# Projections beside an attention stage, in steps of three matmuls behind each of 64 blocks

## Chip, cores and metric

The kernel runs on one core of a Trainium2 chip. The metric is the device time of one execution in microseconds (us), lower is better. The kernel before takes 1805.41 us (median of 3 runs, 1805.12 to 1806.67).

## What is computed

Two layers on 512 tokens of width 1024, everything in float32. Each layer normalizes, projects, and adds three branches: an attention of eight heads in two groups (compressed keys, selected keys, a window), a retention and a causal convolution of 31 taps with a norm of its own. Each branch is projected and multiplied by a gate:

```python
h = _rmsnorm(x, norm_mix[l])
z = h @ w_in[l]
o_nsa = _nsa(q_n, kc, vc, ks, vs, kw, vw, g_n, ...)
o_ret = _retention(q_r, k_r, v_r, g_r, ret_gn[l])
o_conv = _conv_module(c_a, c_b, conv_w[l], ...)
proj = jnp.einsum('bsnc,ncd->bsnd', br, w_branch[l])
gate = jax.nn.sigmoid(m_g).reshape(B, S, N_BRANCH, D_MODEL)
x = x + jnp.sum(gate * proj, axis=2) @ w_out[l]
x = x + jnp.square(jax.nn.relu(_rmsnorm(x, norm_mlp[l]) @ w_ff1[l])) @ w_ff2[l]
```

## The kernel before

Every float32 operand is split into a high and a low part, and each step of 128 rows in a projection is three matmuls (high by high, high by low, low by high) of 128x512. A projection from width 1024 (`proj`) has 8 steps, 24 matmuls; one from width 512 has 4 steps, 12 matmuls. SP loads a block of weights (`wr`), ACT rounds its high part (`wh`, L145), POOL takes the difference (`wl`, L148). PSUM's eight banks are pools by name: three `mm`, two `sc`, two `tp`, one `av`. The program is written for a scheduler that fixes the order of each engine ahead of time; `tc.issue_after(x)` says that what is written under it is to be issued no sooner than instruction x.

In a layer the order is: convolution input and retention, compressed keys and values, keys, values V (four accumulators of 128x280, `proj_tok`), `query(0)`, then the attention. The attention has four head pairs (`attention_pair`, j = 0 to 3), each with four passes (two groups g, two branches br), 16 passes in all. A pass has four blocks (i = 0 to 3), 64 blocks in a layer. For each block PE makes two score matmuls into an `sc` bank (128 to 512 columns), DVE adds the bias and takes the minimum (L712), ACT the exponential (L714). After the fourth block's sum DVE works out the scale (`gate_over`, L627 to L629), ACT applies it to each block (L719), PE transposes the block into a `tp` bank (L722), and ACT and DVE copy it out as high and low part (L727, L728). Eight `av` matmuls end the pass. Each pair also has a small softmax over compressed keys (`pc`, L673 to L690) at its head. `query(j + 1)` is projected during pair j.

DVE also makes the convolution's taps (L338, 0.7 to 0.9 us each), dealt behind the blocks by `conv_taps_behind`; the generator `conv_norm` (L590 to L612) follows from pass 12 on, a piece per pass. What fills PE beside the attention is the list `pending`: eight `mix` items (gate of 24 matmuls, projection of 12) and sixteen `gate_ahead` items (24). One is done before the keys, four (`HELD`) are kept for the end; the other 19 are dealt whole over the passes:

```python
u = 4 * j + k
with tc.issue_after(marks[u].ins):       # the pass's first score matmul
    fill(paced * (u + 1) // 16 - paced * u // 16)
```

Each item ends with a DVE multiply out of its `mm` bank (L448, and L464 for the second half of a `mix`). After the last pass the `os` projections begin, which need all of the attention.

Of the kernel before, what the change touches and what calls it, by code (L numbers as in the profile page):

```python
# [2 lines left out]

# [14 lines left out]
P = 128  # L18
# [3 lines left out]
KC = D // P  # L22
# [11 lines left out]
FB_CA, FB_CB, FB_GR, FB_KC, FB_VC, FB_KS, FB_KW, FB_MG, FB_Q = 0, 4, 8, 12, 13, 14, 15, 16, 40  # L34
# [32 lines left out]
def block_kernel(ctx: ExitStack, tc: tile.TileContext, a, out):  # L67
    nc = tc.nc
# [12 lines left out]
    AHEAD, F_KEYS, HELD = 16, 1, 4  # L81
# [18 lines left out]
    def ps(tag, shape=(P, T)):  # L100
        return tl(psum, tag, PS_BUFS[tag], shape)
# [6 lines left out]
    def mm(o, l, r, start, stop):  # L108
        return nc.tensor.matmul(o, l, r, start=start, stop=stop)  # L109
# [43 lines left out]
    def wblock(src, nk=KC, n=P):  # L153

        return wsplit(raw(lambda t: [(t, src)], nk, n), nk, n)

    def proj(o, w, x, nk=KC):

        h, l = w
        for k in range(nk):  # L160
            xh, xl = x[k]
            mm(o, h[:, k, :], xh, k == 0, False)
            mm(o, h[:, k, :], xl, False, False)
            last = mm(o, l[:, k, :], xh, False, k == nk - 1)
        return last

    def proj_tok(outs, srcs, n, x, shared=1):

# [101 lines left out]
    for l in range(DEPTH):  # L270
# [49 lines left out]
        def conv_taps_behind(ins, n):  # L320
            with tc.issue_after(ins.ins):
                conv_taps(n)
# [118 lines left out]
        merged = [None] * KC  # L441
        gated = set()

        def gate(n, m):
            pg = ps("mm")
            proj(pg, wblock(w_f[FB_MG + n * KC + m]), X)
            t = tl(base, "g", 3)
            nc.vector.tensor_mul(t, pg, rs)  # L448
            nc.scalar.activation(t, t, AF.Tanh, scale=0.5)
            return t  # L450

        def gate_ahead(n, m):
            dma(gdram[n * KC + m], gate(n, m))
            gated.add((n, m))

        def mix(n, o, m):
            if (n, m) in gated:
                t = tl(base, "g", 3)
                dma(t, gdram[n * KC + m])
            else:  # L460
                t = gate(n, m)
            po = ps("mm")
            proj(po, wblock(a["w_b"][l, n, m], 4), o, 4)
            nc.vector.scalar_tensor_tensor(t, t, 1.0, po, op0=OP.add, op1=OP.mult)  # L464
            if n == 1:
                dma(mdram[m], t)
            else:
                nc.vector.tensor_add(merged[m], merged[m], t)

        pending = [lambda m=m: mix(1, RO, m) for m in range(KC)]  # L470
        pending += [lambda k=k: gate_ahead(2 * (k // KC), k % KC) for k in range(AHEAD)]
        paced = len(pending) - F_KEYS - HELD

        def fill(n):
            for _ in range(min(n, len(pending))):
                pending.pop(0)()


        phase.close()
# [84 lines left out]
            conv_taps_behind(low, T_KEYS)  # L564
        G = tl(mix_pool, "G", 1, (P, NB, 24))
        V = []
        pz = [ps(tag) for tag in ("mm", "mm", "mm", "av")]
        proj_tok([p[:, :280] for p in pz], [(a["w_v"][l][:, k0:k0 + nk], nk) for k0, nk in ((0, 3), (3, 3), (6, 2))], 280, X)
        for i in range(NB):
            v = kv((P, 4, P))  # L570
# [80 lines left out]
        def attention_pair(j, tq, more):  # L651
# [43 lines left out]
            for g in range(2):  # L695
                h = g * HPG + j
                nat, oth = halves(g)
                av = ps("av")
                mm(av, vcb[:, g, :], pct, True, False)
                for br in range(2):  # L700
                    den, mx = small((P, NB)), small((P, NB))
                    S = tl(ap, "s", 3, (P, 1280))
                    cols = []
                    for i in range(NB):
                        n = P * (i + 1)
                        sc = ps("sc")
                        m0 = mm(sc[:, :n], QS[g][:, i * P:(i + 1) * P], KHH[br, g][:, :n], True, False)
                        if i == 0:
                            marks.append(m0)
                        mm(sc[:, :n], QS[g][:, i * P:(i + 1) * P], KLL[br, g][:, :n], False, True)  # L710
                        s = S[:, 64 * i * (i + 1):64 * i * (i + 1) + n]
                        nc.vector.tensor_tensor_reduce(s, sc[:, :n], bias[g][:, 384 - 128 * i:512], scale=1.0,  # L712
                                                       scalar=3e38, op0=OP.add, op1=OP.min, accum_out=mx[:, i:i + 1])
                        nc.scalar.activation(s, s, AF.Exp, scale=-1.0, bias=mx[:, i:i + 1], accum_out=den[:, i:i + 1])  # L714
                        cols.append(s)
                    c = gate_over(den, h, 1 + br)
                    ph, pl = tl(ap, "pt", 4, (P, 1280), FR), tl(ap, "pt", 4, (P, 1280), FR)
                    for i in range(NB):
                        nc.scalar.activation(cols[i], cols[i], AF.Copy, scale=c[:, i:i + 1])  # L719
                        pt = ps("tp")  # L720
                        for k in range(i + 1):
                            nc.tensor.transpose(pt[:, k * P:(k + 1) * P], cols[i][:, k * P:(k + 1) * P], ident)  # L722
                        for (vh, ks), (vl, _) in zip(pt_views(ph, i), pt_views(pl, i)):
                            src = pt[:, ks.start * P:ks.stop * P]
                            if len(vh.shape) == 3:
                                src = src.rearrange("p (k q) -> p k q", q=P)
                            nc.scalar.activation(vh, src, AF.Copy)  # L727
                            low = nc.vector.tensor_sub(vl, src, f(vh))  # L728
                        slot = 4 * (4 * j + 2 * g + br) + i
                        conv_taps_behind(low, late_taps * (slot + 1) // T_SLOTS - late_taps * slot // T_SLOTS)  # L730
                    for k, c0 in enumerate((0, 512, 896, 1152)):
                        n = T - k * P
                        lhs = V[k][:, 2 * br + g, :]
                        mm(av[:, k * P:], lhs, ph[:, c0:c0 + n], False, False)
                        mm(av[:, k * P:], lhs, pl[:, c0:c0 + n], False, br == 1 and k == NB - 1)
                    more(j, 2 * g + br)
                t = tmp()
                nc.scalar.activation(t[nat], av[oth], AF.Copy)
                nc.vector.tensor_add(oj[nat], t[nat], av[nat])
            return oj  # L740

        ON, marks, tqs = [], [], [query(0)]
        late_taps = len(todo)

        def more(j, k):

            if k == 0 and j + 1 < HPG:
                tqs.append(query(j + 1))
            if not todo:
                next(normed, None)  # L750
            u = 4 * j + k
            with tc.issue_after(marks[u].ins):
                fill(paced * (u + 1) // 16 - paced * u // 16)

        for j in range(HPG):
            ON.append(attention_pair(j, tqs[j], more))
        conv_taps(len(todo))
        for _ in normed:
            pass
        with tc.issue_after(marks[-1].ins):  # L760
            fill(len(pending))

        phase.close()
        phase = ExitStack()
# [123 lines left out]
```

## Time and profile before

| | |
|---|---|
| median of 3 runs | 1805.41 us |
| the profiled execution, its own time | 1804.74 us |
| its span (first to last instruction) | 1803.0 us |
| mean granted TensorE clock | 0.984 of full |
| PE (matmul) busy | 1757.3 us, 97% |
| DVE busy | 1104.4 us, 61% |
| ACT busy | 774.9 us, 43% |
| POOL busy | 500.6 us, 28% |

Ends of matmuls are modelled, and a matmul that waits in the pipeline counts as busy, so PE's busy time is more than the time it needs; the spacing of starts is a better measure. In layer 0 `query(0)` begins at 205.10 us, the first block is transposed at 241.60, the first `os` projection starts at 465.09; in layer 1 these are 1094.81, 1125.04 and 1348.92.

### The profile page before, as it was taken

What the parts mean: (1) busy time and instruction counts of PE and PEld (TensorE: products, weight loads), DVE (VectorE), ACT (ScalarE), POOL (GpSimd) and SP (SyncE); (2) the same over time, 40 slices, a digit from 0 to 9 for tenths busy, and PEclk for the clock granted to TensorE, in tenths of its full rate; (3) what the DMA queues carried; (4) which work ended last, traced back from release to release, by engine and by line L of the source; (5) the groups of instructions that cost most, each with busy time, mean ns of one, the idle gap of its engine ahead of it and who ended that gap; (6) DMA issues with size and microseconds to landing.
All of it is one profiled execution on the core that took longest, in us unless ns stands there. A gap on an engine that the chain in (4) does not pass through costs nothing.

```text
span 1803.0 us, 23260 instructions
## 1 busy us (share of the span) xinstructions
PE 1757.3 (97%) x8592; PEld 1473.8 (82%) x8592; DVE 1104.4 (61%) x1979; ACT 774.9 (43%) x1421; POOL 500.6 (28%) x420
## 2 busy tenths in 40 slices
PE   8899899989999999999999999999899999999997
PEld 7788788868888888888898888888688888888886
DVE  6976978887554344434459778878857443434344
ACT  4433466766343232323434344667553341323241
POOL 4454444323471000000255543343137500000000
PEclk9999999989999999999999999999899999999998
DMA  4222623221753323333422232332147323332321
GB/s 167 87 88 61 203 94 122 96 71 65 233 169 96 101 96 93 95 96 102 135 94 89 87 127 83 98 131 90 41 161 227 119 94 94 93 94 94 105 85 68
DMA packets 70802, 195.82 MB, mean 109 GB/s; under 512 B 8945, under 2 KB 9329, under 8 KB 70689
## 3 DMA queue, kind: packets, MB, share of 16 engines
q1 hardware_dynamic: 70688, 194.34, 33.6%
q8 instruction: 68, 1.11, 0.3%
q14 instruction: 46, 0.37, 0.1%
HBM read 177.51 MB, written 19.42 MB: 109 GB/s over the span
## 4 chain that ended last, share of the span: by engine, by line
PE 67%; issue 20%; DVE 10%; ACT 2%; DMA 1%; SPq 0%; POOLq 0%; POOL 0%; DVEq 0%; ACTq 0%
PE mm L109 58%; PE sc L109 3%; DVE yc L338 3%; PE av L109 3%; PE tp L722 2%; PE tp L109 1%; DVE XP L500 1%; DVE kv L563 1%; DVE qk L386 1%; ACT s L719 0%; DVE pt L728 0%; ACT wh L145 0%; DVE rr L364 0%; PE tp L190 0%; DVE s L712 0%
## 5 line engine op out<-in xcount | busy, mean ns | idle before, releaser
L109 PE MATMUL mm<-X,wh 128*128 128x512 f32 x2432 | 777.4, 396 | 12.2 <-ACT X L214 6.1
L148 POOL TENSOR_TENSOR wl<-wr,wh 128x512 fp32r<-128x512 f32 (+2 forms) x344 | 436.2, 1290 | 563.2 <-ACT wh L145 540.6
L145 ACT ACTIVATE wh<-wr 128x1024 fp32r<-128x1024 f32 (+2 forms) x301 | 296.9, 987 | 681.9 <-PE mm L109 554.5
L109 PEld LDWEIGHTS mm<-X,wh 128*128 128x128 f32 x2432 | 455.3, 189 | 103.1 <-ACT X L214 6.3
L109 PE MATMUL mm<-X,wl 128*128 128x512 f32 x1216 | 479.5, 394 | 0.4 <-DVE wl L150 0.4
L109 PEld LDWEIGHTS mm<-X,wl 128*128 128x128 f32 x1216 | 230.2, 189 | 46.5 <-DVE wl L150 0.9
L338 DVE SCALAR_TENSOR_TENSOR yc<-u,ccol,yc 128x512 f32<-128x512 f32 x240 | 214.2, 894 | 1.7
L150 DVE TENSOR_TENSOR wl<-wr,wh 128x1024 fp32r<-128x1024 f32 x129 | 158.1, 1225 | 38.4 <-ACT wh L145 38.4
L109 PE MATMUL mm<-fa,wh 128*128 128x512 f32 x512 | 160.2, 395 | 0.0
L109 PE MATMUL mm<-bo,wh 128*128 128x512 f32 x512 | 160.0, 391 | 0.0
L805 DVE SCALAR_TENSOR_TENSOR t<-mm,rs 128x512 f32<-128x512 f32 x64 | 43.9, 691 | 161.5 <-PE mm L109 155.9
L227 POOL TENSOR_TENSOR t<-t,t 128x512 f32<-128x512 f32 x18 | 27.4, 1523 | 333.7 <-DVE wl L150 310.7
L206 POOL TENSOR_TENSOR n<-n,mhalf 128x4 f32<-128x4 f32 x15 | 16.5, 1101 | 372.3 <-DVE n L204 372.3
L109 PE MATMUL mm<-kv,wh 128*128 128x512 f32 x384 | 119.5, 389 | 0.0
L109 PEld LDWEIGHTS mm<-fa,wh 128*128 128x128 f32 x512 | 96.1, 188 | 23.2
L109 PEld LDWEIGHTS mm<-bo,wh 128*128 128x128 f32 x512 | 96.0, 188 | 19.7
L109 PE MATMUL mm<-fa,wl 128*128 128x512 f32 x256 | 100.5, 395 | 0.0
L109 PE MATMUL mm<-bo,wl 128*128 128x512 f32 x256 | 100.2, 392 | 0.0
L714 ACT ACTIVATE s<-s,n 128x128 f32<-128x128 f32 (+3 forms) x128 | 71.4, 559 | 46.9 <-DVE n L712 46.3
L109 PE MATMUL mm<-wh,X 128*128 128x256 f32 (+1 forms) x480 | 90.1, 286 | 0.0
L728 DVE TENSOR_TENSOR pt<-tp,pt 128x128 fp32r<-128x128 f32 (+1 forms) x192 | 70.0, 372 | 32.7 <-ACT pt L727 32.4
L816 DVE TENSOR_TENSOR yc<-yc,mm 128x512 f32<-128x512 f32 x32 | 22.0, 687 | 105.6 <-PE mm L109 105.6
(219 smaller groups left out, 2463.9 us busy)
## 6 DMA issues: line engine op xcount, KB each, us to landing
wr<-in_w_dram SPq DMA_DIRECT2D x128, 512.0 KB, 3.5
wr<-in_w_f_dram SPq DMA_DIRECT2D x87, 512.0 KB, 3.3
wr<-in_w_b_dram SPq DMA_DIRECT2D x48, 256.0 KB, 2.7
wr<-in_w_t_dram SPq DMA_DIRECT2D x16, 512.0 KB, 3.4
gd<-g SPq DMA_DIRECT2D x32, 256.0 KB, 2.0
g<-gd SPq DMA_DIRECT2D x32, 256.0 KB, 2.8
wr<-in_w_o_dram SPq DMA_DIRECT2D x16, 512.0 KB, 3.6
md<-g SPq DMA_DIRECT2D x16, 256.0 KB, 2.9
```

The lines of the kernel that those rows point to most:

```text
L109: return nc.tensor.matmul(o, l, r, start=start, stop=stop)
L145: nc.scalar.activation(h, t, AF.Copy)
L148: nc.gpsimd.tensor_sub(l[:, k], t[:, k], f(h[:, k]))
L150: nc.vector.tensor_sub(l, t, f(h))
L227: (nc.vector if c == KC - 1 or first_time else nc.gpsimd).tensor_add(s, s, acc)
L338: nc.vector.scalar_tensor_tensor(yc[c], x, w, yc[c], op0=OP.mult, op1=OP.add)
L386: nc.vector.tensor_sub(QLr[h][half], pt[nat], f(QHr[h][nat]))
L714: nc.scalar.activation(s, s, AF.Exp, scale=-1.0, bias=mx[:, i:i + 1], accum_out=den[:, i:i + 1])
L722: nc.tensor.transpose(pt[:, k * P:(k + 1) * P], cols[i][:, k * P:(k + 1) * P], ident)
L728: low = nc.vector.tensor_sub(vl, src, f(vh))
L805: nc.vector.scalar_tensor_tensor(t, pf, 0.0, rs, op0=OP.max, op1=OP.mult)
L816: nc.vector.tensor_add(xT[m], xT[m], pf)
```

## The change

`proj` becomes a loop over a generator, `proj_steps`, which yields after each three matmuls. `gate`, `mix` and `gate_ahead` become generators as well. The 19 items (7 `mix` of 12 steps, 12 `gate_ahead` of 8, 180 steps, 540 matmuls) are chained into one generator, `beside`, and 2 or 3 steps are drawn after each of the 64 blocks, to be issued behind that block's last transpose. The four held items follow after the last pass, no longer behind the last pass's first score. V's second and third accumulators take the two `sc` banks in place of two `mm` banks. Line numbers after L160 shift by 5 to 17.

```diff
     def proj(o, w, x, nk=KC):
 
+        for _ in proj_steps(o, w, x, nk):
+            pass
+
+    def proj_steps(o, w, x, nk=KC):
+
         h, l = w
         for k in range(nk):
             xh, xl = x[k]
             mm(o, h[:, k, :], xh, k == 0, False)
             mm(o, h[:, k, :], xl, False, False)
-            last = mm(o, l[:, k, :], xh, False, k == nk - 1)
-        return last
+            mm(o, l[:, k, :], xh, False, k == nk - 1)
+            yield
...
         def gate(n, m):
+            w = wblock(w_f[FB_MG + n * KC + m])
             pg = ps("mm")
-            proj(pg, wblock(w_f[FB_MG + n * KC + m]), X)
+            yield from proj_steps(pg, w, X)
...
-        pending = [lambda m=m: mix(1, RO, m) for m in range(KC)]
-        pending += [lambda k=k: gate_ahead(2 * (k // KC), k % KC) for k in range(AHEAD)]
-        paced = len(pending) - F_KEYS - HELD
+        pending = [(12, mix_steps(1, RO, m)) for m in range(KC)]
+        pending += [(8, gate_ahead(2 * (k // KC), k % KC)) for k in range(AHEAD)]
...
-        pz = [ps(tag) for tag in ("mm", "mm", "mm", "av")]
+        pz = [ps(tag) for tag in ("mm", "sc", "sc", "av")]
...
-                        m0 = mm(sc[:, :n], QS[g][:, i * P:(i + 1) * P], KHH[br, g][:, :n], True, False)
-                        if i == 0:
-                            marks.append(m0)
+                        mm(sc[:, :n], QS[g][:, i * P:(i + 1) * P], KHH[br, g][:, :n], True, False)
...
-                            nc.tensor.transpose(pt[:, k * P:(k + 1) * P], cols[i][:, k * P:(k + 1) * P], ident)
+                            turned = nc.tensor.transpose(pt[:, k * P:(k + 1) * P], cols[i][:, k * P:(k + 1) * P], ident)
...
+                        with tc.issue_after(turned.ins):
+                            for _ in range(paced * (slot + 1) // 64 - paced * slot // 64):
+                                next(beside)
...
+        paced = sum(n for n, _ in pending[:-HELD])
+        beside = itertools.chain(*(steps for _, steps in pending[:-HELD]))
...
-            u = 4 * j + k
-            with tc.issue_after(marks[u].ins):
-                fill(paced * (u + 1) // 16 - paced * u // 16)
...
-        with tc.issue_after(marks[-1].ins):
-            fill(len(pending))
+        for _ in beside:
+            pass
+        del pending[:-HELD]
+        fill(HELD)
```

The first place is PE's order at the head of the attention in layer 0, between the score matmuls of the first two passes (`sc`) and the first block's transpose (`tp<-ident,s`). `mm<-X` and `mm<-bo` are matmuls of the list. Before:

```order
L109 MATMUL sc_393_2200<-kv_337_1882,QS_373_2131 128x384
L109 MATMUL sc_393_2200<-kv_338_1883,QS_373_2131 128x384
L109 MATMUL sc_394_2205<-kv_337_1882,QS_373_2131 128x512
L109 MATMUL sc_394_2205<-kv_338_1883,QS_373_2131 128x512
L690 MATMUL tp_384_2177<-ident_66,pch_383_2174 128x128 x4
L109 MATMUL sc_419_2352<-kv_346_1931,QS_373_2131 128x128
L109 MATMUL sc_419_2352<-kv_347_1932,QS_373_2131 128x128
L109 MATMUL mm_430_2421<-X_12_115,wh_432_2424 128x512
L109 MATMUL mm_430_2421<-X_13_116,wh_432_2424 128x512
L109 MATMUL mm_430_2421<-X_12_115,wl_433_2425 128x512
```

After, up to the first block's transpose and the first matmuls of the list behind it:

```order
L705 MATMUL tp_384_2177<-ident_66,pch_383_2174 128x128 x4
L110 MATMUL sc_421_2357<-kv_346_1931,QS_373_2131 128x384
L110 MATMUL sc_421_2357<-kv_347_1932,QS_373_2131 128x384
L110 MATMUL sc_422_2362<-kv_346_1931,QS_373_2131 128x512
L110 MATMUL sc_422_2362<-kv_347_1932,QS_373_2131 128x512
L110 MATMUL av_387_2185<-pct_385_2182,vc_322_1785 128x512
L110 MATMUL sc_444_2478<-kv_339_1888,QS_375_2136 128x128
L110 MATMUL sc_444_2478<-kv_340_1889,QS_375_2136 128x128
L735 MATMUL tp_398_2217<-ident_66,s_390_2189 128x128
L110 MATMUL mm_402_2229<-X_12_115,wh_400_2224 128x512
L110 MATMUL mm_402_2229<-X_13_116,wh_400_2224 128x512
L110 MATMUL mm_402_2229<-X_12_115,wl_401_2225 128x512
```

Before, 87 matmuls of the list and of the second query stand between `query(0)` and the first block's transpose; now none does, and the first six stand behind that transpose.

The second place is PE's order in pass 10 of layer 0. Before, the list has run out by here, and no matmul of it stands in the 73 rows from the end of pass 9 to that of pass 13:

```order
L722 MATMUL tp_676_3724<-ident_66,s_666_3683 128x128 x3
L109 MATMUL sc_747_4107<-kv_346_1931,QS_708_3935 128x128
L109 MATMUL sc_747_4107<-kv_347_1932,QS_708_3935 128x128
L109 MATMUL sc_748_4112<-kv_346_1931,QS_708_3935 128x256
L109 MATMUL sc_748_4112<-kv_347_1932,QS_708_3935 128x256
L109 MATMUL av_663_3679<-pct_616_3421,vc_322_1785 128x512
L722 MATMUL tp_677_3734<-ident_66,s_666_3683 128x128 x4
L109 MATMUL av_663_3679<-pt_672_3708,kv_364_2068 128x512
L109 MATMUL sc_749_4117<-kv_346_1931,QS_708_3935 128x384
L109 MATMUL sc_749_4117<-kv_347_1932,QS_708_3935 128x384
L109 MATMUL sc_750_4122<-kv_346_1931,QS_708_3935 128x512
L109 MATMUL sc_750_4122<-kv_347_1932,QS_708_3935 128x512
```

After, the same pass, with the list's steps behind each block:

```order
L735 MATMUL tp_680_3738<-ident_66,s_665_3667 128x128 x3
L110 MATMUL mm_679_3730<-X_16_123,wh_677_3725 128x512
L110 MATMUL mm_679_3730<-X_17_124,wh_677_3725 128x512
L110 MATMUL mm_679_3730<-X_16_123,wl_678_3726 128x512
L110 MATMUL mm_679_3730<-X_18_127,wh_677_3725 128x512
L110 MATMUL mm_679_3730<-X_19_128,wh_677_3725 128x512
L110 MATMUL mm_679_3730<-X_18_127,wl_678_3726 128x512
L110 MATMUL sc_711_3926<-kc_307_1699,tq_641_3541 128x64 x4
L110 MATMUL sc_725_3975<-kv_337_1882,QS_707_3916 128x128
L110 MATMUL sc_725_3975<-kv_338_1883,QS_707_3916 128x128
L110 MATMUL av_662_3663<-pct_610_3375,vc_322_1785 128x512
L735 MATMUL tp_681_3754<-ident_66,s_665_3667 128x128 x4
```

Six or nine matmuls of the list now stand behind each block's transposes, in all 64 blocks.

The third place is PE's order where the convolution's norm begins (`mm<-ones` sums columns, `mm<-ident,n` spreads the mean over rows), at the end of pass 13. Before:

```order
L109 MATMUL mm_759_4172<-ones_71,u_737_4063 128x1 x4
L109 MATMUL av_722_3989<-pt_752_4131,kv_364_2068 128x512
L109 MATMUL av_722_3989<-pt_753_4132,kv_364_2068 128x512
L109 MATMUL av_722_3989<-pt_752_4131,kv_365_2072 128x384
L109 MATMUL av_722_3989<-pt_753_4132,kv_365_2072 128x384
L190 MATMUL mm_760_4178<-ident_66,n_758_4171 128x128 x4
L109 MATMUL mm_765_4198<-X_12_115,wh_767_4201 128x512
L109 MATMUL mm_765_4198<-X_13_116,wh_767_4201 128x512
L109 MATMUL mm_765_4198<-X_12_115,wl_768_4202 128x512
L109 MATMUL mm_765_4198<-X_14_119,wh_767_4201 128x512
```

After, from the mean's spreading to the first transpose of pass 14:

```order
L196 MATMUL mm_769_4225<-ident_66,n_767_4218 128x128 x4
L110 MATMUL sc_781_4263<-kv_339_1888,QS_709_3921 128x384
L110 MATMUL sc_781_4263<-kv_340_1889,QS_709_3921 128x384
L110 MATMUL sc_782_4268<-kv_339_1888,QS_709_3921 128x512
L110 MATMUL sc_782_4268<-kv_340_1889,QS_709_3921 128x512
L110 MATMUL av_775_4248<-pct_719_3967,vc_322_1785 128x512
L110 MATMUL sc_801_4374<-kv_348_1937,QS_709_3921 128x128
L110 MATMUL sc_801_4374<-kv_349_1938,QS_709_3921 128x128
L110 MATMUL sc_802_4379<-kv_348_1937,QS_709_3921 128x256
L110 MATMUL sc_802_4379<-kv_349_1938,QS_709_3921 128x256
L735 MATMUL tp_786_4280<-ident_66,s_778_4252 128x128
L110 MATMUL mm_766_4206<-X_14_119,wh_764_4201 128x512
```

Before, a whole gate stands behind the mean's spreading; now the last scores of pass 14 and its first transpose stand there, with no matmul of the list in between.

## Rows read from the trace of the kernel before

**Rows 1.** The page's first lines: span, then busy time by engine
```profile
span 1803.0 us, 23260 instructions
PE 1757.3 (97%) x8592; PEld 1473.8 (82%) x8592; DVE 1104.4 (61%) x1979; ACT 774.9 (43%) x1421; POOL 500.6 (28%) x420
```

**Rows 2.** Busy time by stretch: start and end, length, engines, clock, DMA, GB/s
```profile
205.10:241.60 36.50, 36.09 (x173) 30.38 (x174) 29.92 (x76) 15.40 (x37) 12.29 (x12) 0.91 0.37 117
...
241.60:381.06 139.46, 139.46 (x725) 118.11 (x724) 115.79 (x315) 96.34 (x240) 54.73 (x44) 1.00 0.33 108
...
381.06:412.31 31.25, 24.23 (x112) 18.07 (x110) 27.15 (x77) 19.41 (x55) 2.64 (x2) 0.78 0.08 27
...
1094.81:1125.04 30.23, 29.83 (x142) 24.66 (x141) 24.59 (x66) 15.34 (x36) 12.09 (x12) 0.99 0.27 83
...
1264.30:1296.12 31.82, 25.07 (x112) 18.93 (x110) 27.43 (x77) 19.30 (x55) 2.63 (x2) 0.73 0.08 26
```

**Rows 3.** The chain that ended last: start, length, engine, line, instructions
```profile
455.66 105.57 PE mm L109 x461
```

**Rows 4.** Busy time by stretch of five microseconds, columns as before
```profile
205.00:210.00 5.00, 4.90 (x12) 3.85 (x13) 5.00 (x9) 1.98 (x6) 2.97 (x2) 0.50 0.81 272
210.00:215.00 5.00, 5.00 (x21) 4.06 (x20) 4.82 (x7) 0.64 (x1) 0.59 (x1) 0.87 0.19 54
...
400.00:405.00 5.00, 4.17 (x16) 2.75 (x14) 3.67 (x7) 2.26 (x6) 0.00 (x0) 0.50 0.00 0
...
1090.00:1095.00 5.00, 5.00 (x24) 5.00 (x24) 4.88 (x9) 1.16 (x5) 0.72 (x2) 0.50 0.62 205
```

**Rows 5.** PE's timeline: start, length, operation, idle time before it and releaser
```profile
205.10 1.22 PE L109 MATMUL mm<-X,wh 128*128 128x512 f32 x2 [4.69 <-ACT G L575]
...
395.38 0.66 PE L722 MATMUL tp<-ident,s 128*128 128x128 f32 x4 [1.54 <-DVE pt L728]
...
442.70 0.51 PE L722 MATMUL tp<-ident,s 128*128 128x128 f32 x3
442.97 0.48 PE L109 MATMUL mm<-X,wl 128*128 128x512 f32 x1
```

**Rows 6.** DVE's timeline in layer 0, from the first query to the first gate
```profile
209.24 7.60 DVE L338 SCALAR_TENSOR_TENSOR yc<-u,ccol,yc 128x512 f32<-128x512 f32 x9
...
220.69 0.69 DVE L648 SCALAR_TENSOR_TENSOR tq<-mm,rs 128x512 f32<-128x512 f32 x1
...
230.42 0.68 DVE L448 TENSOR_TENSOR g<-mm,rs 128x512 f32<-128x512 f32 x1
...
234.34 0.69 DVE L712 CUSTOM_DVE_ANT_0 s<-sc,bias 128x512 f32<-128x512 f32 x1
...
236.04 0.67 DVE L627 TENSOR_SCALAR n<-n 128x4 f32<-128x4 f32 x1 [1.00 <-ACT s L714]
...
237.03 0.16 DVE L629 SCALAR_TENSOR_TENSOR n<-G,n 128x4 f32<-128x4 f32 x1
```

**Rows 7.** ACT's timeline, the same place
```profile
235.20 0.71 ACT L714 ACTIVATE s<-s,n 128x512 f32<-128x512 f32 x1
...
237.34 1.91 ACT L719 ACTIVATE s<-s,n 128x128 f32<-128x128 f32 x4
```

**Rows 8.** DVE's timeline, the same place in layer 1
```profile
1104.66 0.68 DVE L648 SCALAR_TENSOR_TENSOR tq<-mm,rs 128x512 f32<-128x512 f32 x1
...
1117.92 0.69 DVE L712 CUSTOM_DVE_ANT_0 s<-sc,bias 128x512 f32<-128x512 f32 x1
...
1120.18 0.69 DVE L627 TENSOR_SCALAR n<-n 128x4 f32<-128x4 f32 x1 [1.57 <-ACT s L714]
...
1121.20 0.16 DVE L629 SCALAR_TENSOR_TENSOR n<-G,n 128x4 f32<-128x4 f32 x1
```

**Rows 9.** DVE's timeline at the convolution's norm in layer 0
```profile
412.59 2.48 DVE L597 TENSOR_TENSOR yc<-yc,mm 128x512 f32<-128x512 f32 x4 [0.31 <-PE mm L190]
...
417.75 0.68 DVE L739 TENSOR_TENSOR on<-t,av 64x512 f32<-64x512 f32 x1 [0.49 <-ACT t L738]
```

More of the change, by code (lines that the diff above doesn't have):

```diff
@@ L1 @@
+import itertools
 import math
@@ L452, in gate_ahead, with mix_steps @@
         def gate_ahead(n, m):
-            dma(gdram[n * KC + m], gate(n, m))
+            t = yield from gate(n, m)
+            dma(gdram[n * KC + m], t)
             gated.add((n, m))
-        def mix(n, o, m):
+        def mix_steps(n, o, m):
             if (n, m) in gated:
@@ L460, in mix @@
             else:
-                t = gate(n, m)
+                t = yield from gate(n, m)
+            w = wblock(a["w_b"][l, n, m], 4)
             po = ps("mm")
-            proj(po, wblock(a["w_b"][l, n, m], 4), o, 4)
+            yield from proj_steps(po, w, o, 4)
             nc.vector.scalar_tensor_tensor(t, t, 1.0, po, op0=OP.add, op1=OP.mult)
@@ L468, in mix @@
                 nc.vector.tensor_add(merged[m], merged[m], t)
-        pending = [lambda m=m: mix(1, RO, m) for m in range(KC)]
-        pending += [lambda k=k: gate_ahead(2 * (k // KC), k % KC) for k in range(AHEAD)]
-        paced = len(pending) - F_KEYS - HELD
+        def mix(n, o, m):
+            for _ in mix_steps(n, o, m):
+                pass
+        pending = [(12, mix_steps(1, RO, m)) for m in range(KC)]
+        pending += [(8, gate_ahead(2 * (k // KC), k % KC)) for k in range(AHEAD)]
         def fill(n):
             for _ in range(min(n, len(pending))):
-                pending.pop(0)()
+                for _ in pending.pop(0)[1]:
+                    pass
         phase.close()
@@ L740, in attention_pair @@
             return oj
-        ON, marks, tqs = [], [], [query(0)]
+        ON, tqs = [], [query(0)]
         late_taps = len(todo)
+        paced = sum(n for n, _ in pending[:-HELD])
+        beside = itertools.chain(*(steps for _, steps in pending[:-HELD]))
         def more(j, k):
@@ L759, in block_kernel @@
             pass
-        with tc.issue_after(marks[-1].ins):
-            fill(len(pending))
+        for _ in beside:
+            pass
+        del pending[:-HELD]
+        fill(HELD)
         phase.close()
```

## The prediction

> **What bounds the kernel now.** I read the page first: PE is busy for 97% of the span, DVE for 61% [rows 1]. So PE's order decides, and time can be won only where PE is starved. The chain that ended last says what a fed PE costs: 461 matmuls in 105.57 us, one every 0.229 us [rows 3]. Next I cut the attention into stretches [rows 2]. In layer 0 three things stand out. At the head, 205.1 to 241.6, PE is busy throughout, and it comes out of a wait of 4.69 us [rows 5]. From 241.6 to 381.1 it never stops, DVE busy for 115.79 of 139.46 us. From 381.06 to 412.31 it is busy for 24.23 of 31.25 us at a granted clock of 0.78: the list of projections has run out, POOL splits no weights (2.64 us), and PE waits for DVE, as at 395.38 [rows 5]. Layer 1 shows the same hole, 31.82 us at 0.73, and a head that is full [rows 2].
>
> The hole is larger than its idle time, since a matmul that waits in the pipeline counts as busy. Its 112 records stream 16x512 + 14x384 + 12x256 + 60x128 = 24,320 columns; at 0.229 us per 512 that is 10.9 us. Narrow ones cost more than their columns: three transposes start within 0.27 us [rows 5], 0.09 each instead of 0.057, so 48 of them add 1.6, twelve other narrow ones 0.4, and the column sums something. I take 13.5 us of work. The hole loses 31.25 - 13.5 = 17.7 us in layer 0 and 31.82 - 13.5 = 18.3 in layer 1; the bounds are 7.0 (its idle time alone) and 20.3 (columns alone).
>
> **The hole is filled: -36.0 us.** The change neither removes nor adds a matmul, a weight load, a DMA or an eviction; it moves them. 540 matmuls go behind 64 blocks, 6 or 9 at each, 1.4 to 2.1 us. Passes 10 to 13 get their share, and while PE runs it, DVE and ACT copy the block out. The whole 17.7 + 18.3 is given back if nothing else starves.
>
> **The head is emptied: +31.3 us.** Those matmuls come from somewhere. Before, 87 of them (19.9 us) stand between the first query and the first block's transpose, and run while DVE and ACT work through the softmax. After, nothing stands there, so PE follows DVE. When does the first transpose come? In layer 0 DVE has four taps fewer ahead of the query's eviction (nine take 7.60 us, 0.84 each [rows 6]), so that starts at 220.69 - 3.4 = 217.3. From there to the last score of pass 0 (234.34 before) DVE loses four pieces of 0.7 us (a second query, its split, two halves of an item) and has four taps put in: +0.6. So that score's sum starts at about 231.6. From it to the scale on ACT is 3.0 us (234.34 to 237.34, by way of exponential and scale [rows 6, 7]), and the first piece takes 0.4: first transpose at 235.0, against 241.6.
>
> PE's work there: before, 241.6 - 200.4 = 41.2 us hold 4.69 of idle time [rows 5], 0.4 more [rows 2], and a half-speed restart. In 205 to 210 the granted clock is 0.50 (1.2 GHz), and 12 matmuls start where 22 would; in 210 to 215 it is 0.87 [rows 4]: 3.0 us in all. That leaves 33.1 us of work, or 13.2 without the 87. After, 13.2 us lie in 34.6, and a restart follows: loss 21.4 + 3.0 = 24.4 against 8.1, so +16.3. V's banks give the first query its bank sooner, and the 4.69 us vanish from where they stand, but the query is not what the transpose waits for.
>
> In layer 1 the query's eviction has the same taps ahead of it and stays at 1104.66. The last score's sum (1117.92) loses five pieces, some 4.5 us with a wait among them, and comes at 1113.4; with 3.0 and 0.4 us behind it the transpose is at about 1117, against 1125.04 [rows 8]. Before, the stretch of 30.23 us lost 0.4 idle and some 0.6 at the half clock that lasted to 1095 [rows 2, 4]. Work: 30.23 - 1.0 - 19.9 = 9.3 us, after in 22.2, a loss of 12.9 + 3.0 against 1.0: +14.9, so +31.2 for both, or 31.3 with the roundings. Bounds: DVE could keep 3 us less or more in each layer (25 to 37), and without a restart it is 6 less.
>
> **Holes inside: +33.2 us.** A pass's first transpose comes 3.5 us after its last score (3.0 and 0.4 as above). Where the order puts enough matmuls between the two, that is hidden; item by item before, whole gates did it. After, I looked for passes where no list matmul stands between them. There are four in each layer:
> - Pass 6: other passes' scores and eight `av` matmuls, 2.7 us of work, in part waiting for `sc` banks themselves: 1.3 us lost.
> - Pass 12: 3.0 us of work: 1.0 lost.
> - Pass 14, at the convolution's norm. The four subtractions (2.48 us), an output addition (0.68) [rows 9] and two sums (1.2) stand on DVE between the mean and the last score's sum; then 1.0 for the exponential, 1.2 for the scale and 0.6 for ACT, with up to three further additions (0.6 each) between: 7.7 us with one of them. Under it PE has 1.4 us of scores: 6.3 lost.
> - Pass 15: the last score is followed by the transpose directly: 3.5 lost.
>
> That is 12.1 us. After such a wait the clock falls, as in 400 to 405 (0.50 [rows 4]); I add 3.0 for pass 14 and 1.5 for pass 15, 16.6 in a layer. Bounds: nothing, if scores run earlier than I think, and 30, if DVE, which is busy for 83% of PE's time in the full stretch [rows 2], falls behind in other passes too.
>
> The rest I cost at nothing. The generators' tails (a multiply on DVE, a tanh on ACT, a store) are as many as before. A block of weights is wanted every third block, some 8 us, and POOL needed 54.73 us of 139.46 for a denser list [rows 2]; if that cover went, PE would wait at the first step of an item, for a few us. The held items lie behind the last pass in both.
>
> The Trainium skill has a rule against this change ("TensorE: Matmul & The Clock Gate", section "Why this matters for your kernels"): idle gaps between bursts of matmuls bring the slow clock back. This case's trace agrees, with 0.50 after the 4.69 us at 205. By the rule an emptied head costs its gap and a slow restart; without the restarts the sum would be 15 us lower.
>
> **Sum.** -36.0 + 31.3 + 33.2 = +28.5. Against the profiled execution's own 1804.74 us that is 1833.2, and the median lies 0.7 above that execution: 1833.5 us.
>
> **Rivals.**
> *A, faster: nothing starves inside.* The passes overlap, and if the scores of a pass are ready a block early, its first transpose finds its data. For it: before, 139 us ran without a stall. Against it: item by item the list covered every gap there, and now four gaps hold none of it. Then the sum is -36.0 + 31.3 = -4.7, 1800.7, and 1795 if one layer's restart is missing too. It decides below 0.5 us of inner loss per layer.
> Beside this rival stands the Trainium skill's "Perfetto Trace Analysis", section "Optimization Strategy": where a kernel has regimes with different busiest engines, interleaving them can help. The trace has such regimes (DVE at the head, PE in the middle).
> *B, no change.* The end's hole has only moved to the head, and inside 2 to 3 us are lost: about 1805. For it: 36.0 and 31.3 are nearly equal.
> *C, much slower: every pass stalls.* A block is followed by at most nine matmuls (2.1 us), the `av` ones add 1.2: 3.3 us against 3.5 and whatever DVE has queued, a tap (0.84) for instance. With 0.9 us lost in each of the other twelve passes that is 2 x 12 x 0.9 = 22 more, 1855.
>
> **How the numbers follow.** My forecast has 0.55, C 0.17, A 0.19, B 0.09. A measurement of this kernel can tell about 0.2%, 3.6 us, from no change: slower 0.72, same 0.09, faster 0.19. The likeliest case alone spans 1820 to 1845; the range, down to A and up to C, is 1799 to 1858.
>
> **What would show it.** PE nearly idle, at half clock, from the first query to a first transpose near 235 and 1117; no hole from pass 10 to 13; waits of PE for ACT's scale ahead of the first transposes of passes 14 and 15. If the first transpose comes as late as 241 the loss is larger, and if passes 14 and 15 run without a wait, A holds.

## The result and the profile after

The changed kernel takes 1831.47 us (median of 4 runs, 1830.20 to 1832.70) where the one before takes 1805.26 (4 runs): 1.0147 times as long, 95% interval 1.0129 to 1.0164. That is 26.2 us more; 28.1 had been forecast. The profiled execution took 1832.70 us, 27.9 more span than before. Its page begins as follows; the other engines' busy times are those of [rows 1] within 1.1 us.

```profile
span 1830.9 us, 23241 instructions
...
PE 1761.5 (96%) x8592; PEld 1472.7 (80%) x8592; DVE 1103.8 (60%) x1979; ACT 775.0 (42%) x1421; POOL 500.5 (27%) x420
```

PE's busy time rose by 4.2 us and its share fell, so most of what was added (27.9 us of span) is time without a matmul. The stretches show where, as [rows 2] did (start and end, length, engines, clock, DMA). In each layer they are: from the end of V's matmuls to the first block's transpose, from there to the first transpose of pass 12, from there to that of pass 15, and from there to the first `os` projection.

```profile
200.77:233.11 32.34, 22.19 (x93) 18.75 (x92) 29.87 (x80) 11.26 (x33) 7.04 (x7) 0.63 0.39 129
233.11:398.30 165.19, 161.94 (x831) 134.07 (x831) 132.26 (x361) 108.68 (x273) 56.82 (x48) 1.00 0.29 95
398.30:443.53 45.23, 38.02 (x191) 31.28 (x192) 25.63 (x68) 26.67 (x64) 12.04 (x9) 0.92 0.20 70
443.53:478.07 34.54, 34.54 (x154) 28.56 (x155) 21.15 (x32) 17.66 (x32) 11.41 (x10) 0.95 0.52 175
1104.78:1131.89 27.11, 15.72 (x59) 12.40 (x58) 23.99 (x70) 11.16 (x32) 6.01 (x5) 0.66 0.23 76
1131.89:1298.08 166.19, 162.78 (x830) 134.74 (x830) 132.11 (x361) 108.63 (x273) 56.80 (x48) 0.99 0.29 94
1298.08:1343.95 45.87, 38.19 (x190) 31.37 (x191) 25.64 (x68) 26.68 (x64) 12.06 (x9) 0.93 0.21 69
1343.95:1376.92 32.97, 32.97 (x155) 27.40 (x155) 21.06 (x32) 17.68 (x32) 11.41 (x10) 1.00 0.55 186
```

Layer 0's `os` projections begin at 478.07 us instead of 465.09, 13.0 later; layer 1's at 1376.92 instead of 1348.92, 28.0 later, 15.0 of it its own. That is the whole loss. The head has become the emptiest stretch (PE busy for 22.19 of 32.34 us at a clock of 0.63, 15.72 of 27.11 at 0.66), and 398 to 444 holds the second: 38.02 of 45.23. The hole of [rows 2] from 381 to 412 is gone.

DVE's timeline at the head of layer 0 (start, length, operation) shows why PE is idle there:

```profile
208.29 5.54 DVE L344 SCALAR_TENSOR_TENSOR yc<-u,ccol,yc 128x512 f32<-128x512 f32 x5
...
217.31 0.69 DVE L663 SCALAR_TENSOR_TENSOR tq<-mm,rs 128x512 f32<-128x512 f32 x1
...
228.83 0.69 DVE L725 CUSTOM_DVE_ANT_0 s<-sc,bias 128x512 f32<-128x512 f32 x1
...
231.25 0.16 DVE L644 SCALAR_TENSOR_TENSOR n<-G,n 128x4 f32<-128x4 f32 x1
```

The query is evicted at 217.31 (220.69 before [rows 6]), the last score of pass 0 is summed at 228.83 (234.34 before), and the scale is ready at 231.4. PE's timeline at that place follows.

```profile
200.77 0.63 PE L110 MATMUL mm<-X,wh 128*128 128x512 f32 x2
...
226.93 3.44 PE L110 MATMUL sc<-kv,QS 128*128 128x384 f32 x8 [3.08 <-DVE n L725]
...
233.11 0.30 PE L735 MATMUL tp<-ident,s 128*128 128x128 f32 x1
233.17 0.71 PE L110 MATMUL mm<-X,wh 128*128 128x512 f32 x2
233.72 0.39 PE L110 MATMUL mm<-X,wl 128*128 128x512 f32 x1
233.95 0.61 PE L110 MATMUL mm<-X,wh 128*128 128x512 f32 x2
```

The query now starts at once, at 200.77 instead of 205.10, and it helps nobody, since DVE comes to it at 217.31. The first transpose is at 233.11. Behind it three matmuls start within 0.78 us, at full speed already. In layer 0 the half clock of the emptied head lay almost wholly under the wait for DVE and ACT. DVE has the scale ready at 231.4, but ACT first ends an exponential of the next pass and copies out `pct`:

```profile
231.82 0.60 ACT L707 ACTIVATE pct<-tp 128x512 fp32r<-128x512 f32 x1
232.32 1.91 ACT L732 ACTIVATE s<-s,n 128x128 f32<-128x128 f32 x4
```

From the start of this scaling to the first transpose it is 0.79 us, where 0.46 is enough when PE waits (443.07 to 443.53 at pass 15); so PE's slow order held the transpose up by some 0.3 us, an estimate. In layer 1 the same is 1.06 us (1130.83 to 1131.89), and there the clock is still low behind the first transpose: the first two matmuls of the list take 1.20 us where the pair at 233.17 took 0.71.

```profile
1131.98 1.20 PE L110 MATMUL mm<-X,wh 128*128 128x512 f32 x2
```

Four stretches of five microseconds show the clock (the last column but two; 0.50 is 1.2 of 2.4 GHz), at the head and behind the stall of pass 14:

```profile
215.00:220.00 5.00, 1.85 (x9) 1.88 (x10) 4.83 (x10) 1.55 (x4) 0.00 (x0) 0.50 0.74 246
...
230.00:235.00 5.00, 5.00 (x23) 4.17 (x23) 2.23 (x11) 4.54 (x14) 0.23 (x1) 0.72 0.09 15
425.00:430.00 5.00, 2.90 (x9) 2.19 (x8) 1.96 (x6) 2.42 (x7) 0.00 (x0) 0.50 0.00 0
430.00:435.00 5.00, 5.00 (x24) 4.03 (x24) 1.05 (x3) 1.30 (x3) 0.00 (x0) 0.93 0.00 0
```

Inside the stage, PE's timeline at passes 14 and 15 (idle time and releaser in brackets):

```profile
423.34 0.50 PE L110 MATMUL av<-pct,vc 128*128 128x512 f32 x1 [2.35 <-DVE on L755]
...
427.33 0.48 PE L735 MATMUL tp<-ident,s 128*128 128x128 f32 x1 [2.10 <-ACT s L732]
...
443.53 0.33 PE L735 MATMUL tp<-ident,s 128*128 128x128 f32 x1 [2.75 <-ACT s L732]
```

PE waits 2.35 us for the output addition that stands on DVE behind the norm's subtractions, 2.10 for the first scaled piece of pass 14 and 2.75 for that of pass 15. Behind pass 14 the clock is low again, 0.50 in 425 to 430 as shown above.

### The profile page after: what moved, and what is told of

Read it like the earlier page. It is cut to its first block, busy times and chain, and to the rows that moved or that the text cites. A ratio compares the mean times of both kernels' runs of the same rounds, so it can differ in the third digit from the quotient of the medians.

```text
span 1830.9 us, 23241 instructions
## 1 busy us (share of the span) xinstructions
PE 1761.5 (96%) x8592; PEld 1472.7 (80%) x8592; DVE 1103.8 (60%) x1979; ACT 775.0 (42%) x1421; POOL 500.5 (27%) x420
## 4 chain that ended last, share of the span: by engine, by line
PE 60%; issue 20%; DVE 15%; ACT 4%; DMA 0%; POOL 0%; SPq 0%; POOLq 0%; DVEq 0%; ACTq 0%
PE mm L110 53%; DVE yc L344 5%; PE sc L110 3%; PE av L110 2%; PE tp L735 1%; ACT s L727 1%; DVE s L725 1%; ACT s L732 1%; DVE pt L741 1%; DVE kv L578 1%; DVE QS L672 1%; DVE XP L515 1%; DVE qk L392 1%; PE tp L110 1%; DVE n L642 0%
## 5 line engine op out<-in xcount | busy, mean ns | idle before, releaser
L212 POOL TENSOR_TENSOR n<-n,mhalf 128x4 f32<-128x4 f32 x15 | 16.5, 1101 | 373.3 <-DVE n L210 373.3
L741 DVE TENSOR_TENSOR pt<-tp,pt 128x256 fp32r<-128x256 f32 (+1 forms) x192 | 71.3, 374 | 71.8 <-ACT pt L740 71.4
L740 ACT ACTIVATE pt<-tp 128x256 fp32r<-128x256 f32 (+1 forms) x192 | 63.0, 338 | 50.3 <-PE tp L735 38.0
```

## The experiments

"The head" is the time from the end of V's matmuls to the first block's transpose, "the stage" the time from there to the first `os` projection. In the changed kernel these are 32.3 and 245.0 us in layer 0, 27.1 and 245.0 in layer 1.

**V's banks alone.** The first run puts V's accumulators back, in the changed kernel:

```diff
-        pz = [ps(tag) for tag in ("mm", "sc", "sc", "av")]
+        pz = [ps(tag) for tag in ("mm", "mm", "mm", "av")]
```

> The changed kernel with V's accumulators back in three mm banks and av. My theory (place of the list's matmuls decides; V's banks are beside the point): the first query waits for a bank again, some 4.7 us, but the first transpose in layer 0 waits for DVE and stays at 233 +- 2, so the time stays at 1831 +- 4. Rival (V's accumulators in the score banks hold up the first scores): 10 us or more faster, under 1822.

1834.90 us (1.0162, 1.0147 to 1.0177): 3.4 us slower than the changed kernel, and the two intervals overlap. PE waits for the bank again:

```profile
206.70 1.09 PE L110 MATMUL mm<-X,wh 128*128 128x512 f32 x2 [4.68 <-ACT G L590]
```

The first transpose comes at 235.68, 2.6 us later and a little later than I expected; V's stage ended 1.1 us later in that execution, which leaves 1.5 for the banks. The rival is dead: V's banks do not hold up the scores.

The opposite edit, in the kernel before:

> The kernel before with only V's second and third accumulators moved to the score banks. My theory: PE is full at the head there, so the 4.7 us wait and its 3.0 us restart at half clock are worth something: 1798 to 1805. Rival (the score banks held by V cost time): 1808 or more.

1809.32 us (10 runs; 1.0024, 1.0014 to 1.0033). I expected a small gain and it is a small loss, on the rival's side; its size is barely over what can be told. Its profiled execution, the fastest of its runs at 1805.67, has a head of 41.4 us as before and stages of 223.9 and 225.1 us (223.5 and 223.9 before). The query's wait is gone there too, but between the query and the first transpose PE then waits 5.7 us in all, where it was 5.1 with the query's own.

**The head filled.** 24 of the 180 steps are drawn behind the four scores of pass 0, the rest is dealt over the blocks:

```diff
+                    for _ in range(behind_scores.get(4 * j + 2 * g + br, 0)):
+                        next(beside)
                     c = gate_over(den, h, 1 + br)
...
-        paced = sum(n for n, _ in pending[:-HELD])
+        behind_scores = {0: 24}
+        paced = sum(n for n, _ in pending[:-HELD]) - sum(behind_scores.values())
```

> The changed kernel with 24 of the 180 steps (72 matmuls, 16.5 us) drawn behind the four scores of pass 0, and the other 156 dealt over the blocks. My theory (the emptied head cost 11 us in layer 0 and 14 in layer 1): the first transpose comes 1 to 4 us later, the head's loss is given back, 1805 +- 6. Rival (it is the cutting into steps of three that costs, wherever they stand): within 5 us of 1831.

1796.67 us (0.9959, 0.9945 to 0.9973): 34.8 us faster than the changed kernel, and faster than the one before. Its stretches (columns as above; head and stage of layer 0, then of layer 1):

```profile
198.22:236.66 38.44, 33.51 (x165) 27.48 (x164) 35.38 (x85) 15.31 (x39) 16.02 (x15) 0.95 0.48 159
236.66:460.19 223.53, 215.12 (x1102) 180.26 (x1103) 173.87 (x454) 148.75 (x361) 73.82 (x59) 0.98 0.30 102
1090.99:1118.73 27.74, 27.44 (x128) 22.57 (x128) 23.29 (x63) 13.84 (x31) 11.59 (x12) 0.97 0.28 92
1118.73:1340.63 221.90, 213.97 (x1104) 179.75 (x1103) 173.12 (x456) 149.64 (x364) 74.39 (x61) 0.98 0.30 105
```

The head of layer 0 grew by 6.1 us and the stage shrank by 21.4; in layer 1 the head stayed (27.7) and the stage shrank by 23.1. The 72 matmuls are 16.5 us of each. Of the other 5 to 7 us, 2 to 3 are idle time of PE inside the stage that went with them (10.3 and 10.9 us in the changed kernel, 8.3 and 7.7 here); the waits at passes 14 and 15 are still there, 7.2 and 7.4 us. The gain is larger than the 26 that I expected, and the rival (steps cost by themselves) is dead.

**Half of it.** `behind_scores = {0: 12}`.

> 12 steps (36 matmuls, 8.2 us) behind the scores of pass 0 in place of 24. My theory (PE idles at the head, and each matmul put there saves its own time in each layer): 16.5 us less work left behind the first transposes of the two layers, 1815 +- 4, about half of the 34.8 us that 24 steps gave. Rival (24 steps gained by clearing pass 6 and 12 of their waits, not by filling the head): under 1805, since these waits go here too.

1822.22 us (1.0101, 1.0086 to 1.0116), worse than the 1815 that I expected, and far from the rival's 1805. The stretches:

```profile
198.44:233.79 35.35, 26.77 (x127) 21.43 (x125) 32.83 (x82) 13.50 (x36) 12.23 (x11) 0.79 0.44 145
233.79:467.92 234.13, 224.91 (x1142) 187.61 (x1141) 178.05 (x456) 150.37 (x364) 79.81 (x63) 0.98 0.30 102
1094.70:1123.75 29.05, 22.41 (x95) 17.58 (x94) 26.11 (x72) 13.68 (x36) 10.00 (x9) 0.88 0.32 106
1123.75:1364.40 240.65, 227.02 (x1140) 188.73 (x1140) 181.97 (x454) 149.88 (x363) 81.83 (x63) 0.97 0.28 99
```

In layer 0 it is as expected: head and stage together take 277.3 us in the changed kernel, 269.5 with 12 steps, 262.0 with 24, that is 0.21 us for each matmul moved to the head (0.229 is its own time [rows 3]). In layer 1 12 steps save 2.4 us and 24 save 22.5. There the order came out otherwise, with waits in the middle passes that layer 0 does not have. One of them, on PE:

```profile
1207.48 0.84 PE L110 MATMUL av<-pt,kv 128*128 128x512 f32 x3 [2.21 <-DVE pt L743]
```

and on DVE just before:

```profile
1204.13 1.82 DVE L344 SCALAR_TENSOR_TENSOR yc<-u,ccol,yc 128x512 f32<-128x512 f32 x1
1205.88 1.22 DVE L644 SCALAR_TENSOR_TENSOR n<-G,n 128x4 f32<-128x4 f32 x1
1207.02 0.41 DVE L743 TENSOR_TENSOR pt<-tp,pt 128x256 fp32r<-128x256 f32 x1
```

The copy-out that PE waits for (`pt`, 1207.02) stands behind a tap and a scale that take 1.82 and 1.22 us here. So moving matmuls to the head saves their time there, but the order of the rest, which the scheduler makes anew each time, can take it back.

**Inside.** 2, 2, 10 and 5 steps behind the scores of passes 6, 12, 14 and 15: `behind_scores = {6: 2, 12: 2, 14: 10, 15: 5}`, in the code above.

> The changed kernel with 2, 2, 10 and 5 of the steps drawn behind the fourth score of passes 6, 12, 14 and 15, the other 161 dealt over the blocks. My theory (the waits ahead of these passes' first transposes, with the clock behind them, are most of what is lost inside, 19 us in a layer): 7 to 10 us back in each layer, 1814 +- 5. Rival (DVE falls behind in every pass, and these four are only where it shows): 1827 or more, the waits turning up at other passes.

1815.88 us (1.0058, 1.0043 to 1.0073), 15.6 us faster than the changed kernel. The two stages:

```profile
230.45:467.07 236.62, 231.07 (x1175) 193.10 (x1175) 179.50 (x458) 151.85 (x368) 82.03 (x67) 0.99 0.31 104
1119.82:1357.47 237.65, 231.56 (x1174) 193.39 (x1175) 179.06 (x458) 151.77 (x367) 82.11 (x67) 0.99 0.30 104
```

They are shorter by 8.3 and 7.4 us. In layer 0 the 2.35 and 2.10 us at pass 14 are under 0.5 and 1.56 now, the 2.75 at pass 15 under 0.5. As expected: these waits and their clock were that much of the loss.

**The steps, dealt as the items were.** The generator stays; 11 or 12 steps a pass are drawn behind its first score (m0), none behind blocks:

```diff
-                        with tc.issue_after(turned.ins):
-                            for _ in range(paced * (slot + 1) // 64 - paced * slot // 64):
-                                next(beside)
...
+            u = 4 * j + k
+            with tc.issue_after(marks[u].ins):
+                for _ in range(paced * (u + 1) // 16 - paced * u // 16):
+                    next(beside)
```

> The changed kernel with the steps of three kept, but drawn as the kernel before drew its items: 11 or 12 steps a pass, behind the pass's first score. PE's order then has 110 projection matmuls ahead of the first transpose again, and none in passes 12 and 13. My theory (the place decides): like the kernel before with V in the score banks, 1803 to 1812. Rival (cutting into steps costs by itself): 1822 or more.

1808.88 us (1.0022, 1.0010 to 1.0033): like the kernel before with V in the score banks (1.0024). Its stages:

```profile
241.58:465.87 224.29, 215.64 (x1092) 179.51 (x1091) 175.56 (x454) 146.25 (x360) 77.04 (x61) 0.98 0.28 96
1126.48:1354.55 228.07, 219.85 (x1093) 183.46 (x1091) 175.71 (x454) 146.25 (x360) 77.03 (x61) 0.96 0.28 95
```

PE's order holds 110 projection matmuls ahead of the first transpose again. So neither the cutting nor the banks cost what was lost; the place does.

**Head and inside together.** 24 steps at the head, and 2, 2, 10 and 5 held behind the last score of passes 6, 12, 14 and 15:

```diff
+                    u = 4 * j + 2 * g + br
+                    with tc.issue_after(scored.ins) if u else ExitStack():
+                        for _ in range(behind_scores.get(u, 0)):
+                            next(beside)
...
+        behind_scores = {0: 24, 6: 2, 12: 2, 14: 10, 15: 5}
```

> 24 steps drawn behind the scores of pass 0, and 2, 2, 10 and 5 steps issued behind the last score of passes 6, 12, 14 and 15, the other 137 over the blocks. My theory (losses at different places add up): the 1796.7 of the run with the head alone, less what the waits at passes 14 and 15 cost (7.2 us idle and some 3 of slow clock in each layer, most of it hidden now): 1782 +- 6. Rival (what the head gives back makes DVE the bound, so the waits move): 1793 or more.

1793.68 us (0.9940, 0.9925 to 0.9955), the fastest of all, but only 3.0 us faster than the head alone: the rival's number. The stage of layer 0 and a piece of it:

```profile
239.06:459.41 220.35, 215.38 (x1103) 178.43 (x1103) 173.11 (x454) 147.63 (x361) 76.49 (x59) 1.00 0.30 102
359.00:389.00 30.00, 29.17 (x155) 23.83 (x154) 28.40 (x87) 21.20 (x55) 8.43 (x6) 1.00 0.28 97
```

The waits at passes 14 and 15 are below 0.5 us, as they should be. But with 137 steps left for 64 blocks DVE is busy for 28.40 of 30 us in one piece, and PE waits elsewhere, mostly for DVE: 4.7 us in layer 0 and 5.7 in layer 1, where the head alone had 1.1 and 0.3 outside of passes 14 and 15 (8.3 and 7.7 with them). So more than half of what was removed came back at other places. What the removal of a wait is worth depends on who is next, and that is mostly DVE.

Small differences between these runs need care. V's last matmul stands ahead of everything that was moved, and still it starts at 198.1 us in the run with the head alone and at 201.2 here; 3.1 us of the comparison arise ahead of the change.

**A little less in each place.** `behind_scores = {0: 20, 14: 6, 15: 4}`.

> 20 steps behind the scores of pass 0, 6 and 4 behind the last score of passes 14 and 15, the other 150 over the blocks. Between the run with the head alone and the one with head and inner places. If DVE's pace in the middle passes is what holds the latter (28.4 of 30 us busy in one stretch), more matmuls per block there are free and this is as fast or faster: 1789 to 1795. If the matmuls at the head and at the end are what counts, it is slower: 1797 or more.

1814.32 us (1.0056, 1.0039 to 1.0073), slower by 20.6 us than the run that it stands next to. By the expectation the matmuls at head and end count; but four steps fewer at the head are 2.8 us a layer. PE's idle time in the stage is 10.5 us in layer 0 and 10.8 in layer 1, where the run next to it has 4.7 and 5.7. The edit also took the steps at passes 6 and 12 away, four of ten at pass 14 and one of five at pass 15. At pass 14 PE now has 18 matmuls of the list between last score and first transpose, where the run next to it has 33, and it waits (3.81 us in layer 1):

```profile
422.34 0.47 PE L739 MATMUL tp<-ident,s 128*128 128x128 f32 x1 [3.85 <-ACT s L736]
```

DVE and ACT show what stands in the chain here:

```profile
417.63 0.67 DVE L456 TENSOR_TENSOR g<-mm,rs 128x512 f32<-128x512 f32 x1
418.23 0.67 DVE L616 TENSOR_TENSOR u<-u,u 128x512 f32<-128x512 f32 x1
418.92 1.14 DVE L642 TENSOR_SCALAR n<-n 128x4 f32<-128x4 f32 x1
```

```profile
417.14 1.05 ACT L146 ACTIVATE wh<-wr 128x1024 fp32r<-128x1024 f32 x1
```

An item's end falls in this place: its multiply (`g<-mm,rs`) and the rounding of the next weights on ACT (1.05 us, ahead of the last exponential) delay the scale (`n`), with the norm's additions (`u<-u,u`) between. From the last score's sum to the scale it is 5.4 us, against 3.6 in the run next to it, where an item's multiply stands in this place as well. So the wait has two parts: 1.8 us of a longer chain and 15 matmuls (3.4 us) less to cover it. The other idle time is in waits of up to 1.8 us in earlier passes. Head and stage together are 12.9 and 9.0 us longer than in the run next to it, of which the idle time in the stage is 5.8 and 5.1; a lower granted clock goes with the rest (0.92 and 0.98 in head and stage of layer 0, against 0.97 and 1.00).

**The norm taken out of the way.** `conv_norm` runs after the last pass:

```diff
-            if not todo:
-                next(normed, None)
```

> The changed kernel with the convolution's norm taken out of passes 13 to 15 and run after the last pass, beside the four held items. Steps and banks stay; PE's order then has 33 and 42 matmuls of the list between last score and first transpose in passes 14 and 15. My theory (the norm's DVE pieces stand in the way of pass 14's scores, and the order makes up for it): the waits of 7.2 us and their slow clock go in each layer, 1815 +- 5. Rival (the norm only moves to the end and stalls the next projections as much): 1827 or more.

1833.32 us (1.0159, 1.0144 to 1.0175): my expectation failed, the rival holds. The 7.2 us of waits at passes 14 and 15 are gone, and PE has this at the end instead:

```profile
449.99 1.86 PE L110 MATMUL mm<-ones,u 128*128 128x1 f32 x8 [7.75 <-DVE u L616]
453.20 1.12 PE L196 MATMUL mm<-ident,n 128*128 128x128 f32 x4 [1.34 <-POOL n L212]
```

The norm's column sums stand ahead of the held items on PE, and wait 7.75 us for DVE, then 1.34 for POOL, with the half clock behind. The wait has moved.

With the head filled as well (24 steps, 5 and 5 behind the last scores of passes 14 and 15):

> The norm after the last pass, 24 steps behind the scores of pass 0, 5 and 5 behind the last score of passes 14 and 15, the other 146 over the blocks. My theory: the gains of the head (35 us) and of the norm's move add up, 1780 +- 7. Rival (DVE bound): 1793 or more.

1816.81 us (1.0070, 1.0055 to 1.0085), not 1780; the same wait is 6.06 us in layer 0, 6.07 in layer 1, and further ones of about 1 us appear in the middle passes. PE's idle time in the stage is 12.8 and 14.2 us, against 8.3 and 7.7 with the head alone.

**V's banks with the head filled.** The head's run with V in three `mm` banks.

> The run with 24 steps at the head, with V's accumulators back in three mm banks. If V's banks are worth nothing either way: 1796.7 +- 3. If the score banks held by V cost some 4 us, as the kernel before with V moved suggests: 1792. If they save 3 us, as the changed kernel suggests: 1800.

1801.34 us (10 runs; 0.9985, 0.9976 to 0.9995), 4.7 us slower than with V in the score banks (0.9959, 0.9945 to 0.9973). The query waits 5.0 us in layer 0 and starts at 206.84. The traces do not put all of it on the banks. From V's end to the first `os` projection the profiled execution is 1.3 us longer in layer 0 and 0.3 in layer 1; 3.8 of its 5.5 us arise ahead of that, where V's last matmul starts at 201.86 instead of 198.09. In the runs with V in the score banks that start lies anywhere from 198.1 to 201.7. So the banks are worth 1 to 2 us here, and the rest is not shown to be theirs.

## Why the prediction was right

The sum was right within 2 us, and the places were the right ones, but the terms missed on both sides and the misses cancelled; that part is luck. By the account below the head cost 24.7 us where I had forecast 31.2, and the inside 38.9 where I had forecast 33.2. The sum has two slips as well: 1833.2 and 0.7 make 1833.9, not 1833.5, and rival A's 1795 needs both layers' restarts to be missing, not one.

*The head* was forecast at +16.3 and +14.9 us. DVE's way to it was right to the start: 217.3 forecast for the query's eviction, 217.31 measured. From there to the last sum I took 14.3 us, measured 11.5: the taps put in there take 0.74 us each, not the 0.84 of [rows 6], the second query's split, which I took off at 0.7, had taken 1.35, and two waits of DVE (0.38 us for a DMA, 0.31 for ACT) fell away; the rest is in small operations. From the last sum to the first transpose I took 3.4 us, measured 4.3 in layer 0 and 4.6 in layer 1: 0.9 of it is ACT's, which has other pieces ahead of the scaling. The first transpose came at 233.11, not 235.0.

The restart of 3.0 us, which I put behind the first transpose of each layer, was not paid there in layer 0, where the clock was back by then. In layer 1 it was paid in part: the granted clock is 0.68 from 1131.89 to 1135.00, about 1 us.

So layer 0's head cost 32.2 - 13.2 - 8.1 = +10.9 (32.2 from V's end at 200.9 to 233.11). In layer 1 the transpose came 6.1 us earlier than 13.0 us of shift would have it; without the 19.9 us of matmuls that is +13.8. Filling the head gave back more than this, 34.8 us in both layers: the rest came from the stages, which shrank by 4.9 and 6.6 us more than the 72 matmuls take. Together with the steps dealt by pass (1808.88), that shows the place of the matmuls as the cause, with the head as the one place that gave back most.

*The hole* was given back: no stretch in passes 10 to 13 stands idle any more. Its -17.7 and -18.3 cannot be measured apart from what follows.

*Inside* I forecast 16.6 us a layer. The stages grew by 21.5 and 21.2 us; less 19.9 us of matmuls moved in, plus the hole as forecast, that is 19.3 and 19.6. Of the four places, pass 14 lost 4.5 us (6.3 forecast), pass 15 2.75 (3.5), pass 12 1.2 (1.0), pass 6 0.3 (1.3); and the clock behind passes 14 and 15 some 3 more. That leaves some 7 us a layer. PE's idle time shows about 2 of them, in waits of 0.2 to 0.5 us in other passes; the rest may be matmuls that waited in the pipeline, or the hole may have given back less than I took. No run here has taken that apart. Rival C, with 11 us a layer in the other passes, is not borne out by idle time. The run with the four places filled gave back 15.6 us of the 38.9 in both layers.

*The rivals.* A said that nothing would starve inside; it fell on passes 14 and 15. The regimes that I named beside it are not those of [rows 2]: at the head PE is busy for 36.09 of 36.50 us and DVE for 29.92, and only in the hole is DVE ahead, 27.15 against 24.23. B said that the end's hole merely moved; the hole (36.0) and what filling the head gave back (34.8) are near each other, but the head's own loss was 24.7, and the waits inside came on top. The clock's rule, that an idle gap between bursts slows PE afterwards (the Trainium skill, "TensorE: Matmul & The Clock Gate", section "Why this matters for your kernels"), agrees with 0.50 in 215 to 220 and in 425 to 430. What it cost differs: behind the stall of pass 14, where PE had matmuls of the list to run, it cost their time; at the head, where PE waited for DVE and ACT, some 0.3 us in layer 0 and some 0.6 in layer 1, and about 1 us more behind the first transpose of layer 1.

Left open: why the kernel before loses some 4 us with V in the score banks, and where the changed kernel loses the 5 us a layer that show as no idle time.

## What to carry to other kernels

Dealing filler evenly is right only if the need for it is even. Count first where the engine would starve (here a head of 30 us and two passes with a norm on DVE's chain) and put the filler there; 72 matmuls moved to each layer's head turned +26 us into -8. And when a scheduler makes the order, look at the new order after each small move: with four steps fewer at the head and nine fewer at the other places a layer, the fastest kernel became 20.6 us slower. New idle time in the stages is 10.9 us of that, and 7.7 of it stands at pass 14, which had less to cover a chain that an item's tail made longer.

## What the hardware showed that I had not expected

The slow clock behind a gap can be nearly free: at the head of layer 0 it was 0.50 from 210 to 230, and PE's first matmuls behind the first transpose ran at full pace. It need not be: in layer 1, with the same program, the clock came back later, and the first pair behind the transpose took 1.20 us where it took 0.71 in layer 0. No run tried what decides between the two.

And a DVE operation of one shape (a tap, 128x512) took between 0.73 and 1.73 us in one head (five in 5.54 us at 208.29, single ones in 0.74, one in 1.73 at 201.27); what stretches it was not tried.
